# RWKV-7 chunk inverses on VectorE in a PSUM bank, merged in place by 32-row tiles, and token-shift mixes kept in DRAM

## The chip, the cores and the metric

The kernel runs on one core of a Trainium2 chip. The metric is the device time of one execution in microseconds. PE is TensorE, DVE is VectorE, ACT is ScalarE, POOL is GpSimd, and SP is the engine whose queue issues the transfers. Each engine works through its own instructions in order; a wait holds all that stand behind it on that engine.

## The reference

Two layers over 512 tokens of width 1024, in float32. Layer 0 is RWKV-7 time mixing with 16 heads of 64, layer 1 differential attention; both end with a gated per-layer embedding. The change lies in layer 0:

```python
xmix = xn[None] + (x_prev - xn)[None] * mu[:, None, None, :]
rkvg = jnp.einsum('cbsd,cde->cbse', xmix[:4], w_in)
r, k, v, g = rkvg[0], rkvg[1], rkvg[2], rkvg[3]
...
def step(state, inp):
    r_t, w_t, k_t, v_t, kk_t, a_t = inp
    s_kk = jnp.einsum('bhij,bhj->bhi', state, kk_t)
    state = (state * w_t[:, :, None, :]
             - s_kk[..., None] * (kk_t * a_t)[:, :, None, :]
             + v_t[..., None] * k_t[:, :, None, :])
    return state, jnp.einsum('bhij,bhj->bhi', state, r_t)
```

## The kernel before

**Dense work.** A float32 product is made of three fast matmuls (`mm3`, L277 to L279) of values split into a high and a low part. The four projections r, k, v, g of layer 0 have two halves of 512 output columns each; `ORDER` lists the eight. Each half takes eight steps over the input width, one step four groups of three 128x512 matmuls. A step needs a split weight tile (`w_split`: a copy on ACT or DVE by L262, then the low part by L310 on POOL or DVE) and a mix. `mix` forms x + (x_prev - x) mu for 128 channels: ACT scales into a PSUM bank (L472), DVE adds the shifted term there (L474), ACT copies the high part (L478), DVE forms the low part (L480). Both halves of a projection form the same mix anew, 64 in all; two buffers for even and two for odd steps hold them.

**Chunks.** The recurrence goes in chunks of 64 tokens, eight of them, for two groups of eight heads. `gram` forms for two chunks at once the masked products of keys and queries, in G. Each chunk and head then needs the inverse of a 64x64 unit triangular matrix. `inverse` makes 32 of them at once (four chunks of one group), so there are four calls, here numbers 0 and 1 (group 0), 2 and 3 (group 1). Each 64x64 matrix has two 32x32 diagonal blocks and one below. The diagonal blocks are inverted by substitution, 31 steps of one multiplication (L903) and one addition (L906), all blocks side by side; `SUBST` gives the engine: POOL for 0, 1 and 2, DVE for 3. DVE brings blocks into and out of that layout by 32x32 transposes (L895, L912, L929). Then the block below is made by two products ("merge", L947 and L960), with operands set into zeroed 64-wide tiles (memsets L934 to L937 on POOL, copies on ACT), and the result is put together in a tile X.

**Recurrence.** For each chunk PE runs L1033 (state), L1043 (G), L1059 (the inverse X), L1072 (state update) and L1078 (output), with copies on ACT between (L1056, L1064, L1098) and the state's update on DVE (L1092, L1095). `finish` normalises and gates a block of 128 tokens and head group (L1118 to L1168, DVE and POOL).

**Order.** All work is written as generators. `Streams` runs a plan while the program is built: each step yields an engine and a cost, the earliest start goes next, and the order in which steps are taken is the order of the instructions on each engine. Where a step may go to either of two engines, `PREF` is an allowance for the first one. After the projections come, on one stream, the embedding's product, the output projection and layer 1.

Of the kernel before, what the change touches and what calls it, by code (L numbers as in the profile page):

```python
# [198 lines left out]
def yoco_kernel(ctx: ExitStack, tc: tile.TileContext, I, out):  # L199
    nc = tc.nc  # L200
    k = Core(tc, ctx)
    cp = k.const
# [56 lines left out]
    ENG = {"ACT": nc.scalar, "DVE": nc.vector, "Pool": nc.gpsimd}  # L259

    def copy(dst, src):
        (nc.scalar.copy if sc.eng == "ACT" else ENG[sc.eng].tensor_copy)(dst, src)  # L262
# [197 lines left out]
    def mix(key, hf, par):  # L460

        c = MIX[key]
        for d in range(par, NT, 2):
# [8 lines left out]
            nc.scalar.activation(m, x_at(d), AF.Copy, scale=omm[:, c, d : d + 1])  # L472
# [1 line left out]
            nc.vector.scalar_tensor_tensor(  # L474
                m[:, 1:], x_at(d)[:, 0 : S - 1], vcol(V_MU + c, d), m[:, 1:], ALU.mult, ALU.add
            )
# [1 line left out]
            nc.scalar.copy(h, m)  # L478
# [1 line left out]
            nc.vector.tensor_sub(l, m, h.bitcast(F32))  # L480
# [389 lines left out]
    def inverse(n):  # L870

        g, cp = batches[n]
        for u in range(2):
# [13 lines left out]
        for q, r in enumerate(quads):  # L887
            for hd, src in lower(q, 32 * (q % 2)):
                yield "ACT/DVE+", (0.24, 0.2)
                copy(na[r, hd], src)  # L890
# [6 lines left out]
        eng = SUBST[g][cp]  # L897
        ve = ENG[eng]
        base, rate = {"DVE": (0.19, 0.00105), "Pool": (0.21, 0.0024)}[eng]
        for s_ in range(31):  # L900
# [2 lines left out]
            ve.tensor_mul(  # L903
                tmp[:, 0:m, 0:w], bc(xs[:, s_ : s_ + 1, 0:w], [P, m, w]), bc(nb[:, s_ + 1 : 32, s_ : s_ + 1], [P, m, w])
            )
            ve.tensor_add(xs[:, s_ + 1 : 32, 0:w], xs[:, s_ + 1 : 32, 0:w], tmp[:, 0:m, 0:w])  # L906
# [5 lines left out]
        nc.vector.transpose(xr, bc(xs.unsqueeze(3), [P, 32, 16, 2]))  # L912
# [17 lines left out]
        yield "take", "R", 3  # L930
        bdc, bdw = R([P, 16, HN]), R([P, 16, HN])
        Xc = X[g, cp] = R([P, 16, HN])
        yield "Pool", 0.89
# [4 lines left out]
        for par in range(2):
            q, c0 = 2 - 2 * par, 32 * (1 - par)
            for hd, src in lower(q, 32):  # L940
                yield "ACT/DVE+!", (0.24, 0.2)
                copy(bdc[quads[q], hd, c0 : c0 + 32], src)
        yield "take", "pw", 1
        ps = bank("pw")
        yield "PE", 1.67, 0.5
        for hd in range(16):
            nc.tensor.matmul(ps[0:64, 32 * hd : 32 * hd + 32], bdc[:, hd, :], xT[:, hd, :], start=True, stop=True)  # L947
        yield "ACT", 1.18
        for j in range(2):
            nc.scalar.copy(bdw[quads[2 * j + 1], :, quads[j]], pv_(ps, 32)[quads[j]])  # L950
        yield "free", "pw", 1
        yield "free", "R", 2
        yield "ACT!", 2.5
        for j, q in enumerate(quads):
            nc.scalar.copy(Xc[q, :, 32 * (j % 2) : 32 * (j % 2) + 32], x32[q])
        yield "take", "pw", 1
        ps = bank("pw")
        yield "PE", 1.67, 0.5
        for hd in range(16):
            nc.tensor.matmul(ps[0:64, 32 * hd : 32 * hd + 32], bdw[:, hd, :], x32[:, hd, :], start=True, stop=True)  # L960
        yield "ACT", 1.18
        for j in range(2):
            nc.scalar.copy(Xc[quads[2 * j], :, 32:64], pv_(ps, 32)[quads[j]])
        yield "free", "pw", 1
        yield "free", "H", 2
# [828 lines left out]
```

## Time and profile before

| | us |
|---|---|
| median of 3 runs (lowest, highest) | 887.76 (884.79, 887.78) |
| profiled execution | 888.55 |
| its span | 886.8 |

The span runs from the first to the last instruction; 1.75 us of the profiled time lie around it. In the views, each engine's busy time does not count waits; a wait is put down to what ended it, so "PE p L279 <- POOL R L310" is time in which PE stood at line 279 until POOL's instruction of line 310 was done. "PEclk" is the granted TensorE clock as a share of full speed. Tiles H and R are buffers in SBUF, p is a PSUM bank, RAW an unsplit weight.

### The profile page before, as it was taken

What the parts mean: (1) busy time and instruction counts of PE and PEld (TensorE: products, weight loads), DVE (VectorE), ACT (ScalarE), POOL (GpSimd) and SP (SyncE); (2) the same over time, 40 slices, a digit from 0 to 9 for tenths busy, and PEclk for the clock granted to TensorE, in tenths of its full rate; (3) what the DMA queues carried; (4) which work ended last, traced back from release to release, by engine and by line L of the source; (5) the groups of instructions that cost most, each with busy time, mean ns of one, the idle gap of its engine ahead of it and who ended that gap; (6) DMA issues with size and microseconds to landing.
All of it is one profiled execution on the core that took longest, in us unless ns stands there. A gap on an engine that the chain in (4) does not pass through costs nothing.

```text
span 886.8 us, 13629 instructions
## 1 busy us (share of the span) xinstructions
PE 809.3 (91%) x4968; PEld 666.3 (75%) x4968; DVE 614.0 (69%) x1243; ACT 515.0 (58%) x1135; POOL 304.3 (34%) x419
## 2 busy tenths in 40 slices
PE   6989999079999997679999999999999999999996
PEld 3767776057888886567878888888888888888885
DVE  3999987177665889895636668548886268863744
ACT  3888569158654775345634456449775378753531
POOL 3545418994251788674520001002100012210100
PEclk9998999579999997799999999999999999999998
DMA  7331220031121144025514444332022321324402
GB/s 284 106 96 60 74 95 0 0 127 42 61 72 49 60 159 138 1 72 193 163 56 147 141 127 158 95 95 67 30 95 72 96 71 50 101 90 157 140 14 95
DMA packets 31203, 83.12 MB, mean 94 GB/s; under 512 B 4128, under 2 KB 8608, under 8 KB 31136
## 3 DMA queue, kind: packets, MB, share of 16 engines
q1 hardware_dynamic: 31136, 82.25, 28.3%
q8 instruction: 39, 0.64, 0.3%
q14 instruction: 28, 0.23, 0.1%
HBM read 73.85 MB, written 8.39 MB: 93 GB/s over the span
## 4 chain that ended last, share of the span: by engine, by line
PE 68%; DVE 14%; POOL 7%; ACT 6%; issue 3%; DMA 2%; DVEq 0%; SPq 0%; POOLq 0%
PE p L277 16%; PE p L279 16%; PE p L278 16%; POOL H L906 2%; POOL H L903 2%; PE p L1600 2%; PE p L848 2%; PE p L1043 1%; PE p L1033 1%; PE p L1267 1%; ACT R L262 1%; PE p L1565 1%; PE p L1059 1%; PE p L1564 1%; DVE p L474 1%
## 5 line engine op out<-in xcount | busy, mean ns | idle before, releaser
L279 PE MATMUL p<-R,R 128*128 128x512 f32 x800 | 316.4, 396 | 25.5 <-POOL R L310 25.3
L277 PE MATMUL p<-R,R 128*128 128x512 f32 x800 | 328.7, 411 | 4.3 <-ACT R L478 2.0
L278 PE MATMUL p<-R,R 128*128 128x512 f32 x800 | 315.2, 394 | 3.7 <-DVE R L480 3.6
L279 PEld LDWEIGHTS p<-R,R 128*128 128x128 f32 x800 | 151.8, 190 | 60.1 <-POOL R L310 26.2
L277 PEld LDWEIGHTS p<-R,R 128*128 128x128 f32 x800 | 152.2, 190 | 36.7 <-ACT R L478 3.6
L278 PEld LDWEIGHTS p<-R,R 128*128 128x128 f32 x800 | 152.3, 190 | 31.7 <-DVE R L480 5.2
L310 POOL TENSOR_TENSOR R<-RAW,R 128x512 fp32r<-128x512 f32 x46 | 63.5, 1386 | 112.5 <-ACT R L262 61.3
L310 DVE TENSOR_TENSOR R<-RAW,R 128x512 fp32r<-128x512 f32 x94 | 67.4, 728 | 27.3 <-ACT R L262 25.2
L316 DVE SCALAR_TENSOR_TENSOR R<-RAW,vec,R 128x512 fp32r<-128x512 f32 x64 | 46.5, 747 | 32.0 <-ACT R L314 31.7
L262 ACT CAST R<-RAW 128x512 fp32r<-128x512 f32 x102 | 61.5, 619 | 5.4 <-DMA RAW<-in_w_v 2.2
L1254 POOL TENSOR_TENSOR hr<-hm,half 128x1 f32<-128x1 f32 x16 | 11.1, 693 | 147.8 <-DVE hm L1252 147.8
L474 DVE SCALAR_TENSOR_TENSOR p<-R,vec,p 128x511 f32<-128x511 f32 x64 | 48.1, 756 | 12.2 <-ACT p L472 11.9
L478 ACT CAST R<-p 128x512 fp32r<-128x512 f32 x64 | 37.7, 589 | 31.4 <-DVE p L474 30.8
L480 DVE TENSOR_TENSOR R<-p,R 128x512 fp32r<-128x512 f32 x64 | 43.4, 682 | 7.7 <-ACT R L478 7.5
L903 POOL TENSOR_TENSOR H<-H,R 128x126 f32<-128x126 f32 (+22 forms) x93 | 40.0, 430 | 24.4 <-PE p L664 20.7
L472 ACT ACTIVATE p<-R,omm 128x512 f32<-128x512 f32 x64 | 44.4, 693 | 3.4 <-DVE R L452 2.3
L314 ACT ACTIVATE R<-RAW,vec 128x512 fp32r<-128x512 f32 x64 | 44.6, 723 | 2.6 <-DMA RAW<-in_b_w_in 2.1
L906 POOL TENSOR_TENSOR H<-H,H 128x126 f32<-128x126 f32 (+22 forms) x93 | 39.2, 422 | 7.3
L1576 ACT ACTIVATE H<-p,mx 128x128 f32<-128x128 f32 (+3 forms) x64 | 33.4, 527 | 8.0 <-DVE mx L1573 6.4
L1569 DVE CUSTOM_DVE_ANT_0 p<-p,cmask 128x128 f32<-128x128 f32 (+3 forms) x64 | 30.5, 506 | 6.9 <-PE p L1565 6.7
L262 ACT CAST R<-R 64x512 fp32r<-64x512 f32 (+1 forms) x37 | 22.9, 618 | 20.9 <-DVE R L1160 16.4
L996 ACT COPY R<-p 128x128 f32<-128x128 f32 x64 | 12.3, 278 | 35.3 <-PE p L993 35.2
(225 smaller groups left out, 1453.9 us busy)
## 6 DMA issues: line engine op xcount, KB each, us to landing
RAW<-in_ple_gate SPq DMA_DIRECT2D x16, 512.0 KB, 3.5
RAW<-in_kv_w SPq DMA_DIRECT2D x16, 512.0 KB, 3.4
RAW<-in_b_w_in SPq DMA_DIRECT2D x16, 512.0 KB, 3.5
R<-in_x SPq DMA_DIRECT2D x8, 512.0 KB, 5.9
RAW<-in_w_r SPq DMA_DIRECT2D x8, 512.0 KB, 3.4
RAW<-in_w_k SPq DMA_DIRECT2D x8, 512.0 KB, 3.4
RAW<-in_w_v SPq DMA_DIRECT2D x8, 512.0 KB, 3.4
RAW<-in_w_g SPq DMA_DIRECT2D x8, 512.0 KB, 3.4
```

What stands on the lines that cost most here:

```text
L262: (nc.scalar.copy if sc.eng == "ACT" else ENG[sc.eng].tensor_copy)(dst, src)
L277: nc.tensor.matmul(ps, ah, bh, start=first, stop=False)
L278: nc.tensor.matmul(ps, ah, bl, start=False, stop=False)
L279: nc.tensor.matmul(ps, al, bh, start=False, stop=last)
L310: ENG[sc.eng].tensor_sub(lo, f, hi.bitcast(F32))
L314: nc.scalar.activation(hi, f, AF.Copy, scale=g)
L316: nc.vector.scalar_tensor_tensor(lo, f, g, hi.bitcast(F32), ALU.mult, ALU.subtract)
L472: nc.scalar.activation(m, x_at(d), AF.Copy, scale=omm[:, c, d : d + 1])
L474: nc.vector.scalar_tensor_tensor(m[:, 1:], x_at(d)[:, 0 : S - 1], vcol(V_MU + c, d), m[:, 1:], ALU.mult, ALU.add)
L480: nc.vector.tensor_sub(l, m, h.bitcast(F32))
L903: ve.tensor_mul(tmp[:, 0:m, 0:w], bc(xs[:, s_ : s_ + 1, 0:w], [P, m, w]), bc(nb[:, s_ + 1 : 32, s_ : s_ + 1], [P, m, w]))
L906: ve.tensor_add(xs[:, s_ + 1 : 32, 0:w], xs[:, s_ + 1 : 32, 0:w], tmp[:, 0:m, 0:w])
```

## The change

Three parts, and two settings of the plan.

- **Substitution.** Numbers 0, 2 and 3 run on DVE, number 1 on POOL. On DVE the unknowns `xs` lie in a PSUM bank (ACT copies the identity there), so that each of the 62 instructions has one input in the bank and one in SBUF, and the additions write to the bank.
- **Merge.** The zeroed tiles, the memsets and X are gone. Each merge is 32 products of 32x32 blocks (two for each matrix pair, in different rows and columns of the array) where it was 16 of 128x64 by 32, taken from G and from the substitution's result as they lie. The inverse is written back into G, by 16 copies of 32x128 on ACT or DVE and 8 on ACT, and the recurrence reads it there (L1059 becomes L1081).
- **Mixes.** The first half of each projection forms its mixes and stores each to DRAM (`mD`, 512 KB each, 32 stores); the second half loads them (32 loads).
- **Plan.** v's first half now comes before r's second; `PREF` is 0; POOL's cost in the substitution is raised.

```diff
-ORDER = [("r", 0), ("k", 0), ("r", 1), ("v", 0), ("k", 1), ("v", 1), ("g", 0), ("g", 1)]
+ORDER = [("r", 0), ("k", 0), ("v", 0), ("r", 1), ("k", 1), ("v", 1), ("g", 0), ("g", 1)]
+FIRST = [(k, h) for n, (k, h) in enumerate(ORDER) if k not in [x for x, _ in ORDER[:n]]]
-PREF = 0.4
+PREF = 0.0
-SUBST = (("Pool", "Pool"), ("Pool", "DVE"))
+SUBST = (("DVE", "Pool"), ("DVE", "DVE"))
...
+            if (key, hf) not in FIRST:
+                yield "wait", ("kept", key, d)
+                yield "DMA", 1.7
+                nc.sync.dma_start(t.bitcast(F32), mD[c, d])
+                yield "set", ("mix", key, hf, d)
+                continue
...
             yield "set", ("mix", key, hf, d)
+            yield "DMA!", 1.7
+            nc.sync.dma_start(mD[c, d], t.bitcast(F32))
+            yield "set", ("kept", key, d)
...
+        if eng == "DVE":
+            yield "take", "pw", 1
+            eye, xs = xs, bank("pw").rearrange("p (s c) -> p s c", c=16)
+            yield "ACT!", 0.52
+            nc.scalar.copy(xs, eye)
...
-        nc.gpsimd.memset(bdc, 0.0)
-        nc.gpsimd.memset(bdw, 0.0)
-        nc.gpsimd.memset(Xc, 0.0)
...
-            nc.tensor.matmul(ps[0:64, 32 * hd : 32 * hd + 32], bdc[:, hd, :], xT[:, hd, :], start=True, stop=True)
+            for j in range(2):
+                block = lower(2 * j, hd // 8, hd // 4 % 2)[:, hd % 4, 32:64]
+                nc.tensor.matmul(
+                    ps[j][quads[2 * j + 1], 32 * hd : 32 * hd + 32], block, xT[quads[2 * j], hd, :], start=True, stop=True
+                )
...
+        for u in range(2):
+            for hh in range(2):
+                sl = slice(8 * u + 4 * hh, 8 * u + 4 * hh + 4)
+                for q in range(4):
+                    yield "ACT/DVE+!", (0.2, 0.2)
+                    copy(lower(q, u, hh)[:, :, 32 * (q % 2) : 32 * (q % 2) + 32], x32[quads[q], sl])
```

The plan comes out in another order. On DVE, where substitution 0 ends, before (L474 and L480 are mixes, L586 to L590 centre v; H_1073 holds the unknowns that POOL works on):

```order
L480 TENSOR_TENSOR R_1422<-p_1423,R_1422 128x512 [waits PE_49,Activation_49]
L474 SCALAR_TENSOR_TENSOR p_1452<-R_113,vec_83,p_1452 128x511 [waits Activation_49]
L480 TENSOR_TENSOR R_1451<-p_1452,R_1451 128x512 [waits PE_49,Activation_49]
L912 STREAM_TRANSPOSE R_1523<-H_1073 128x1024 [waits DMAHW5_49,Pool_49]
L586 TENSOR_REDUCE vmean_88<-H_1524 128x8 [waits Activation_49]
L586 TENSOR_REDUCE vmean_88<-H_1528 128x8 [waits Activation_49]
L588 TENSOR_SCALAR vmean_88<-vmean_88 128x8
L590 TENSOR_TENSOR H_1432<-H_1432,vmean_88 128x512 [waits DVE_49]
```

and in the changed kernel (p_1011 is the bank, L923 and L926 are the substitution, L313 a weight split, L932 to L943 bring the result back):

```order
L923 TENSOR_TENSOR H_1001<-p_1011,R_1102 128x3x15 [waits DVE_49]
L926 TENSOR_TENSOR p_1011<-p_1011,H_1001 128x3x15 [waits DVE_49]
L923 TENSOR_TENSOR H_1001<-p_1011,R_1102 128x2x15 [waits DVE_49]
L926 TENSOR_TENSOR p_1011<-p_1011,H_1001 128x2x15 [waits DVE_49]
L313 TENSOR_TENSOR R_1445<-RAW_1303,R_1445 128x512 [waits Activation_49]
L923 TENSOR_TENSOR H_1001<-p_1011,R_1102 128x16 [waits DVE_49]
L926 TENSOR_TENSOR p_1011<-p_1011,H_1001 128x16 [waits DVE_49]
L932 STREAM_TRANSPOSE R_1476<-p_1011 128x1024 [waits DMAHW1_49,DMAHW7_49,DVE_49,PE_49]
L941 TENSOR_SCALAR H_1489<-R_1476,rowm_100 128x32x16 [waits DVE_49]
```

The transpose of the result waited for POOL with v's and the next mixes behind it; now it follows the substitution on DVE itself, with weight splits between the last steps, and no mixes stand there.

On SP, before, while v's first half is loaded (L293 loads a weight, L561 one of the decay's):

```order
L293 DMA RAW_899<-in_w_v 128x1024 [waits DMAHW3_49,DVE_49,Pool_49]
L293 DMA RAW_928<-in_w_v 128x1024 [waits DMAHW4_49,DVE_49,Pool_49]
L293 DMA RAW_975<-in_w_v 128x1024 [waits DMAHW6_49,DVE_49,Pool_49]
L293 DMA RAW_1000<-in_w_v 128x1024 [waits DMAHW7_49,Pool_49]
L293 DMA RAW_1052<-in_w_k 128x1024 [waits DMAHW0_49,DVE_49,Activation_49]
L561 DMA H_1120<-in_w2a 128x512
```

and in the changed kernel while r's second half is loaded (L296 loads a weight, L493 stores a mix, L475 loads one):

```order
L493 DMA mD<-R_959 128x1024 [waits DMAHW7_49,DVE_49]
L296 DMA RAW_1042<-in_w_r 128x1024 [waits DMAHW4_49,Activation_49,Pool_49]
L475 DMA R_1051<-mD 128x1024 [waits DMAHW1_49,PE_49]
L493 DMA mD<-R_1007 128x1024 [waits DVE_49]
L475 DMA R_1088<-mD 128x1024 [waits DMAHW3_49,PE_49]
L296 DMA RAW_1111<-in_w_k 128x1024 [waits DMAHW6_49,DVE_49,Pool_49]
```

Between two weight loads now stand stores that wait for DVE and loads of mixes that wait for PE to free their buffer.

On PE, in one step of group 1's recurrence, before, between the product with G (L1043) and the product with the inverse (L1059); L993 and L1154 are transposes for other chunks:

```order
L1043 MATMUL p_3509<-R_3414,R_2550 64x64
L993 MATMUL p_3519<-ident_85,R_1190 128x128
L993 MATMUL p_3519<-ident_85,R_1195 128x128
L993 MATMUL p_3519<-ident_85,R_1374 128x128
L993 MATMUL p_3519<-ident_85,R_1709 128x128
L1154 MATMUL p_3533<-ident_85,R_2194 128x128 x4
L1059 MATMUL p_3509<-H_3529,R_3249 64x64 x8
```

and in the changed kernel, between the same two (L1065 and L1081), during g's first half (L280 to L282 are the dense matmuls):

```order
L1065 MATMUL p_3164<-R_2511,R_2390 64x64
L280 MATMUL p_2863<-R_2980,R_2787 128x512
L281 MATMUL p_2863<-R_2980,R_2787 128x512
L282 MATMUL p_2863<-R_2980,R_2787 128x512
L280 MATMUL p_2841<-R_2994,R_2837 128x512
L281 MATMUL p_2841<-R_2994,R_2837 128x512
L282 MATMUL p_2841<-R_2994,R_2837 128x512
L1081 MATMUL p_3164<-H_3181,R_2389 64x64
```

Group 1's recurrence stands beside g's two halves now, where before most of it stood after them; so dense matmuls of g lie between its products.

More of the change, by code (lines that the diff above doesn't have):

```diff
@@ L49 @@
 INVP = (0.5, 0.5, 0.5, 0.5)
-SUBST = (("Pool", "Pool"), ("Pool", "DVE"))
+SUBST = (("DVE", "Pool"), ("DVE", "DVE"))
+RUN = ((1, 1), (1, 1))
 QP, UEP, L1P, PLEP = 4, 5, 7, 8
@@ L212, in yoco_kernel @@
     hD = dram.tile([NB, P, D], F32, name="hD")
+    mD = dram.tile([4, NT, P, 2, S], F32, name="mD")
     ring = ctx.enter_context(pool("ring"))
@@ L818, in yoco_kernel @@
     AOFF, ROFF = (64, 0), (0, 64)
-    G, X, UV, YT = {}, {}, {}, {}
+    G, UV, YT = {}, {}, {}
     heads = [(ii, hh) for ii in range(4) for hh in range(2)]
@@ L872, in inverse, with lower @@
         g, cp = batches[n]
-        for u in range(2):
-            yield "wait", ("gram", 2 * cp + u, g)
-        def lower(q, c):
+        def lower(q, u, hh):
             par = 1 - q // 2
-            off = AOFF[par] + c
-            for n, (u, hh) in enumerate(((0, 0), (0, 1), (1, 0), (1, 1))):
-                yield slice(4 * n, 4 * n + 4), G[2 * cp + u, hh, g][quads[q], :, par, off : off + 32]
+            return G[2 * cp + u, hh, g][quads[q], :, par, AOFF[par] : AOFF[par] + HN]
+        yield "wait", ("gram", 2 * cp, g)
+        eng = SUBST[g][cp]
+        ve = ENG[eng]
         yield "take", "H", 3
@@ L886, in inverse @@
         nc.sync.dma_start(xs, I["eye32"])
[L887 to L890, printed above, removed]
+        if eng == "DVE":
+            yield "take", "pw", 1
+            eye, xs = xs, bank("pw").rearrange("p (s c) -> p s c", c=16)
+            yield "ACT!", 0.52
+            nc.scalar.copy(xs, eye)
+            yield "free", "H", 1
+        for u in range(2):
+            yield "wait", ("gram", 2 * cp + u, g)
+            for hh in range(2):
+                for q, r in enumerate(quads):
+                    yield "ACT/DVE+!", (0.2, 0.2)
+                    copy(na[r, 8 * u + 4 * hh : 8 * u + 4 * hh + 4], lower(q, u, hh)[:, :, 32 * (q % 2) : 32 * (q % 2) + 32])
         yield "take", "R", 1
@@ L896, in inverse @@
         yield "free", "H", 1
-        eng = SUBST[g][cp]
-        ve = ENG[eng]
-        base, rate = {"DVE": (0.19, 0.00105), "Pool": (0.21, 0.0024)}[eng]
+        base, rate = {"DVE": (0.19, 0.00105), "Pool": (0.24, 0.0024)}[eng]
+        late = 0.09 if eng == "DVE" else 0.08
+        cost = [2 * base + 2 * rate * (31 - s_) * (s_ // 2 + 1) for s_ in range(31)]
         for s_ in range(31):
             m, w = 31 - s_, s_ // 2 + 1
-            yield eng + "+", 2 * base + 2 * rate * m * w - base / 2
+            if s_ % RUN[g][cp] == 0:
+                yield "DVE" if eng == "DVE" else "Pool+", sum(cost[s_ : s_ + RUN[g][cp]]) - late
             ve.tensor_mul(
@@ L912, in inverse @@
         nc.vector.transpose(xr, bc(xs.unsqueeze(3), [P, 32, 16, 2]))
-        yield "free", "H", 1
-        yield "take", "H", 2
-        x32, xT = HT([P, 16, 32]), HT([P, 16, 32])
+        yield ("free", "pw", 1) if eng == "DVE" else ("free", "H", 1)
+        yield "take", "H", 3
+        x32, xT, w32 = (HT([P, 16, 32]) for _ in range(3))
         xv = x32.rearrange("p h t -> p t h")
@@ L925, in inverse @@
         fl = lambda t: t.rearrange("p a j -> p (a j)")
-        pv_ = lambda ps, j: ps.rearrange("p (a j) -> p a j", j=j)
         yield "DVE", 0.6
         nc.vector.transpose(fl(xT), fl(x32))
[L930 to L933, printed above, removed]
-        nc.gpsimd.memset(bdc, 0.0)
-        yield "Pool!", 1.78
-        nc.gpsimd.memset(bdw, 0.0)
-        nc.gpsimd.memset(Xc, 0.0)
[L938 to L942, printed above, removed]
@@ L943, in inverse @@
-        yield "take", "pw", 1
-        ps = bank("pw")
+        yield "take", "pw", 2
+        ps = [bank("pw") for _ in range(2)]
         yield "PE", 1.67, 0.5
         for hd in range(16):
-            nc.tensor.matmul(ps[0:64, 32 * hd : 32 * hd + 32], bdc[:, hd, :], xT[:, hd, :], start=True, stop=True)
+            for j in range(2):
[3 more added lines that the diff above has]
+                )
@@ L948, in inverse @@
         yield "ACT", 1.18
         for j in range(2):
[L950 to L957, printed above, removed]
+            r = quads[2 * j + 1]
+            nc.scalar.copy(w32[r], ps[j][r].rearrange("p (a j) -> p a j", j=32))
@@ L958, in inverse @@
+        yield "free", "pw", 2
+        yield "take", "pw", 2
+        ps = [bank("pw") for _ in range(2)]
         yield "PE", 1.67, 0.5
         for hd in range(16):
[L960 to L965, printed above, removed]
+            for j in range(2):
+                r = quads[2 * j + 1]
+                nc.tensor.matmul(
+                    ps[j][quads[2 * j], 32 * hd : 32 * hd + 32], w32[r, hd, :], x32[r, hd, :], start=True, stop=True
+                )
@@ new lines, in inverse @@
+        for u in range(2):
+            for hh in range(2):
+                sl = slice(8 * u + 4 * hh, 8 * u + 4 * hh + 4)
+                for q in range(4):
+                    yield "ACT/DVE+!", (0.2, 0.2)
+                    copy(lower(q, u, hh)[:, :, 32 * (q % 2) : 32 * (q % 2) + 32], x32[quads[q], sl])
+        for u in range(2):
+            for hh in range(2):
+                sl = slice(8 * u + 4 * hh, 8 * u + 4 * hh + 4)
+                for j in range(2):
+                    yield "ACT!", 0.2
+                    nc.scalar.copy(
+                        lower(2 * j, u, hh)[:, :, 32:64], ps[j][quads[2 * j]].rearrange("p (a j) -> p a j", j=32)[:, sl]
+                    )
@@ L966, in inverse @@
+        yield "free", "pw", 2
+        yield "free", "H", 3
         yield "set", ("prep", g, cp)
@@ L1059, in recur @@
                 nc.tensor.matmul(
-                    pA[U, cols(ii, hh)], X[g, cq // 2][:, 8 * (cq % 2) + 4 * hh + ii, :], gt[:, cols(ii, hh)],
+                    pA[U, cols(ii, hh)], G[cq, hh, g][:, ii, par, AOFF[par] : AOFF[par] + HN], gt[:, cols(ii, hh)],
                     start=True, stop=True, skip_group_check=True,
```

3 lines of the change are left out of this document (removed).

## The prediction

> **What bounds the kernel now.** I read the busy shares and slices of the page first, then busy time by stage, then who made PE wait in the two stages that stand out.
>
> ```profile
> PE 809.3 (91%) x4968; PEld 666.3 (75%) x4968; DVE 614.0 (69%) x1243; ACT 515.0 (58%) x1135; POOL 304.3 (34%) x419
> PE   6989999079999997679999999999999999999996
> ```
> PE is the bound over the whole, with two holes: slices 7 and 8 (155 to 200 us) and 15 to 17 (333 to 399). By stage (columns: length, busy us of PE, PEld, DVE, ACT, POOL with instruction counts, then the granted clock, DMA share and GB/s):
>
> ```profile
> 20.00:100.00 80.00, 72.54 (x328) 56.81 (x327) 78.64 (x112) 62.10 (x112) 39.59 (x32) 0.96 0.23 73
> 140.00:160.00 20.00, 14.59 (x59) 10.16 (x57) 12.50 (x18) 16.50 (x34) 17.69 (x40) 0.96 0.00 0
> 160.00:180.00 20.00, 2.26 (x5) 1.83 (x6) 4.35 (x8) 0.00 (x0) 18.20 (x47) 0.50 0.06 18
> 180.00:200.00 20.00, 13.96 (x77) 10.74 (x75) 13.83 (x22) 11.86 (x31) 18.61 (x31) 0.77 0.36 127
> 200.00:320.00 120.00, 117.85 (x1110) 100.37 (x1109) 86.69 (x148) 77.60 (x178) 56.60 (x90) 1.00 0.21 64
> 340.00:360.00 20.00, 11.68 (x119) 10.83 (x120) 19.45 (x39) 9.45 (x22) 15.86 (x15) 0.57 0.12 41
> 360.00:380.00 20.00, 14.30 (x145) 12.66 (x144) 15.57 (x37) 7.22 (x19) 9.44 (x11) 0.84 0.00 1
> 380.00:400.00 20.00, 15.40 (x164) 12.70 (x163) 19.47 (x36) 9.25 (x25) 16.86 (x15) 0.93 0.26 81
> 100.00:409.00 309.00, 257.33 (x2083) 213.31 (x2083) 229.03 (x388) 181.16 (x405) 185.25 (x295) 0.91 0.23 73
> 440.00:880.00 440.00, 437.19 (x2262) 366.31 (x2261) 279.10 (x684) 245.03 (x568) 52.48 (x61) 1.00 0.30 96
> ```
> Hole A (140 to 200): 5.4+17.7+6.0 = 29.2 us idle, and the busy part at clocks 0.96, 0.50 and 0.77 loses 0.6+1.1+3.2 = 4.9 more: 34. Hole B (340 to 400): 18.6 idle and 5.0+2.3+1.1 = 8.4 by the clock: 27. With dense work beside a recurrence (200 to 320) only 2.2 of 120 is idle, and nothing is to be had after 440.
>
> Two marks in time, group 0's first recurrence matmul and the first dense one after the gates:
>
> ```profile
> 205.83 1.15 PE L1043 MATMUL p<-R,R 128*64 128x64 f32 x16
> 409.30 0.40 PE L277 MATMUL p<-R,R 128*128 128x512 f32 x1
> ```
> Hole A, PE's and DVE's longest waits (total, times, longest) and POOL's rows around them:
>
> ```profile
> PE p L279 <- POOL R L310: 25.3, 2, 20.5
> DVE R L912 <- POOL H L906: 20.6, 2, 19.5
> 130.30 0.29 POOL L903 TENSOR_TENSOR H<-H,R 128x31 f32<-128x31 f32 x1 [20.66 <-PE p L664]
> 175.33 0.22 POOL L906 TENSOR_TENSOR H<-H,H 128x16 f32<-128x16 f32 x1
> 176.42 1.27 POOL L310 TENSOR_TENSOR R<-RAW,R 128x512 fp32r<-128x512 f32 x1
> ```
> Substitution 0 runs on POOL from 130.30 to 175.55, interleaved with number 1. A weight split (L310) stands behind it, and PE waits for that split; DVE stands at the transpose L912, with the mixes queued behind. Hole B:
>
> ```profile
> PE p L1072 <- ACT R L1064: 5.0, 3, 3.7
> PE p L1033 <- DVE R L1095: 4.7, 4, 1.5
> PE p L947 <- ACT R L262: 3.1, 1, 3.1
> ```
> These are links of group 1's recurrence. Each step of it is a chain of small products, copies and state updates, PE has too little dense work to put between them, and its clock falls as well (0.57 from 340 to 360), which makes the small products slower still.
>
> **The change, part by part.** *Substitution 0 to DVE.* In DVE's order, shown with the change, the transpose L912 waited for POOL; as L932 it follows DVE's own last addition, and weight splits stand inside the substitution. Hole A goes whole: -34. DVE's price comes from these rows (timeline: start, length; then groups: busy, mean ns; then min/median/max ns):
>
> ```profile
> 362.25 0.28 DVE L903 TENSOR_TENSOR H<-H,R 128x120 f32<-128x120 f32 x1
> 362.57 0.28 DVE L906 TENSOR_TENSOR H<-H,H 128x120 f32<-128x120 f32 x1
> 387.48 0.17 DVE L903 TENSOR_TENSOR H<-H,R 128x16 f32<-128x16 f32 x1
> 387.69 0.17 DVE L906 TENSOR_TENSOR H<-H,H 128x16 f32<-128x16 f32 x1
> L906 DVE TENSOR_TENSOR H<-H,H 128x126 f32<-128x126 f32 (+22 forms) x31 | 18.4, 595 | 1.1
> L903 DVE TENSOR_TENSOR H<-H,R 128x126 f32<-128x126 f32 (+22 forms) x31 | 13.8, 444 | 0.4
> L310 DVE TENSOR_TENSOR R<-RAW,R x94: 641/691/1540, 40.9 to 855.3; 128x512 fp32r<-128x512 f32 x94
> L480 DVE TENSOR_TENSOR R<-p,R x64: 637/684/694, 25.2 to 345.2; 128x512 fp32r<-128x512 f32 x64
> L474 DVE SCALAR_TENSOR_TENSOR p<-R,vec,p x64: 710/746/1373, 22.8 to 342.9; 128x511 f32<-128x511 f32 x64
> L704 DVE SCALAR_TENSOR_TENSOR R<-H,H x8: 661/683/1719, 55.3 to 208.7; 128x512 f32<-128x512 f32 x8
> ```
> Undisturbed, one starts 0.32 us after the last at 120 elements and 0.21 at 16: 0.193 + 0.00105 per element. With 62 instructions and 5,712 elements that is 18.0 us. The one substitution that DVE ran took 18.4+13.8 = 32.2, since POOL was working beside it. With one input in a bank L480 never passed 0.694, where L310, both inputs in SBUF, reached 1.540; so I expect the undisturbed price, plus 0.063 for each of the 31 additions written back to the bank (L474's 746 against L704's 683): 20 us. Bounds 18 and 32; I take the value near the lower end because the row nearest in kind, L480, is the one that POOL doesn't stretch.
>
> [...]
>
> *Mixes from DRAM.* Of 64 mixes 32 go:
>
> ```profile
> L474 DVE SCALAR_TENSOR_TENSOR p<-R,vec,p 128x511 f32<-128x511 f32 x64 | 48.1, 756 | 12.2 <-ACT p L472 11.9
> L480 DVE TENSOR_TENSOR R<-p,R 128x512 fp32r<-128x512 f32 x64 | 43.4, 682 | 7.7 <-ACT R L478 7.5
> hD<-R SPq DMA_DIRECT2D x4, 512.0 KB, 2.6
> R<-hD SPq DMA_DIRECT2D x4, 512.0 KB, 5.5
> ```
> DVE loses 32 x 1.438 = 46 us, gains 3x20-32 = 28 for the substitutions, and some 22 operations of 0.69 that POOL did (15): -3, so about 226 us of work in a stage 36 shorter than 309, 83% full. That is hidden behind PE, not a gain of its own. Before 100 us nothing changes: the first 24 mixes are still formed, and DVE is full (78.64 of 80). The 64 added transfers of 512 KB go through SP's queue (its order is shown with the change). Weights and fetches now stand behind stores that wait for DVE. A fetch lands in some 5.5 us, and PE has three steps of twelve 0.23 us matmuls (8.2 us) before it needs it, so it costs nothing unless SP is held over 2.7 us; I take 0 to 10, inside the new waits below.
>
> *Merges by 32-row tiles.* PE issues 64 instructions of 32x32 for 32 before, eight times:
>
> ```profile
> 195.03 2.02 PE p L947 x32
> 219.93 0.62 PE p L1072 x16
> ```
> L1072 alternates between halves of the array, 0.039 apiece in its run; L947, which doesn't, 0.063. So 64 cost 2.5 to 4.0 us, 0.5 to 2.0 more, in all +4 to +16, all on PE. I take +10, since successive tiles differ but change weights each time. POOL's twelve memsets and ACT's part of 32 mixes go too; neither engine is waited for there any more, so I cost that at nothing.
>
> *Recurrence earlier.* In PE's order before, small matmuls alone stand between L1043 and L1059 of a group 1 step; after it, six dense ones stand between L1065 and L1081. These (1.4 us) now cover the copy that L1059 waited for. So B behaves like 200 to 320: -27.
>
> *New waits.* PE stands at four merges, as it stood 3.1 us at L947. Copies into G now follow each second merge, 24 small ones before the recurrence starts. And substitution 1 stays on POOL, with its L932 on DVE ahead of key and split work:
>
> ```profile
> L903 POOL TENSOR_TENSOR H<-H,R 128x126 f32<-128x126 f32 (+22 forms) x93 | 40.0, 430 | 24.4 <-PE p L664 20.7
> L906 POOL TENSOR_TENSOR H<-H,H 128x126 f32<-128x126 f32 (+22 forms) x93 | 39.2, 422 | 7.3
> ```
> That is at least 31 x 0.852 = 26 us on POOL, and 45 if as stretched as number 0 was. I take +15 for all of it (four merges at about 2.5, and 5 for SP and L932); ends 4 and 30.
>
> Sum against the profiled execution, 888.55 (span 886.8 and 1.75 around it): 888.5-34-27+10+15 = 852.5. The median of the runs is 0.8 lower, so 852.
>
> **Rivals.** *DVE becomes the bound* (slower). If its substitutions cost 32 as the traced one did, DVE has 226+36 = 262 us; at 83% full the stage takes 316 instead of 309, and the time is 888+7 = 895. For it speaks DVE's 98% before 100 us, against it L480's steady 0.69. It decides from about 31 us each.
> *Hole B stays*: the recurrence is bound by its own links whatever stands between: 852+27 = 879. Against it speaks 200 to 320, where steps with dense work cost no idle time.
> *POOL's remaining substitution holds DVE*: hole A moves to L932 of number 1, at up to the 19.5 us seen: 872. The order puts two state updates ahead of it, which speaks against.
> *No new waits, and merges no dearer*: 888-61+4 = 831, down to 826 with nothing at all left over. [...]
>
> **How the numbers follow.** Likeliest (838 to 866, predicted 852): 0.50. No new waits (826 to 838): 0.18. Hole B stays or L932 holds (866 to 883): 0.20. Both, about as before: 0.05. DVE-bound: 0.07. The range 826 to 882 leaves about 0.15 out. A change of 0.5%, 4.4 us, is about what a measurement can tell from none: faster 0.88, same 0.05, slower 0.07.
>
> **What would show it.** Right: no PE wait for a POOL split near 160; L923+L926 on DVE at 0.27 to 0.35 us each and none over 0.7; the first recurrence matmul, at 205.8 before, near 165; the dense work after the gates, at 409.3 before, from about 373; merges of 64 in 2.5 to 4 us. Wrong: the substitutions near 0.5 us an instruction; DVE idle behind POOL at L932; PE waiting for DMA into a mix; or PE at clock 0.5 to 0.8 anywhere between 140 and 370.

## The result, and the profile after

The changed kernel takes 855.1 us (median of 4 runs, 852.11 to 855.45) beside 886.4 us for the kernel before on the same chip: a ratio of 0.964, 95% interval 0.961 to 0.967. The prediction was 852. The profiled execution took 855.45 us, span 853.7. PE's rows of the page:

```profile
PE 810.8 (95%) x5224; PEld 668.3 (78%) x5224; DVE 614.7 (72%) x1399; ACT 461.9 (54%) x1051; POOL 200.5 (23%) x250
PE   6897999999899699898999999999999999999996
```
The two holes have closed; what is left are single slices of 6 to 8 tenths, spread out. Busy time by stage (columns as in the prediction):

```profile
20.00:100.00 80.00, 69.24 (x262) 53.83 (x261) 71.48 (x102) 56.41 (x99) 28.17 (x25) 0.86 0.53 191
100.00:140.00 40.00, 40.00 (x250) 32.50 (x249) 35.01 (x76) 20.12 (x44) 9.94 (x9) 0.93 0.60 209
160.00:180.00 20.00, 20.00 (x216) 16.23 (x215) 14.80 (x22) 14.13 (x35) 18.07 (x34) 1.00 0.58 219
220.00:240.00 20.00, 18.05 (x177) 15.21 (x178) 13.64 (x29) 13.49 (x36) 3.50 (x4) 0.66 0.46 146
280.00:300.00 20.00, 13.36 (x67) 9.70 (x65) 18.61 (x48) 7.51 (x16) 6.36 (x7) 0.82 0.59 218
340.00:360.00 20.00, 17.20 (x245) 14.79 (x244) 11.37 (x16) 11.76 (x37) 14.58 (x15) 0.91 1.03 344
380.00:400.00 20.00, 17.22 (x143) 14.30 (x143) 16.13 (x28) 8.90 (x19) 9.23 (x10) 0.91 0.44 144
```
From 160 to 180, where PE had 2.26 us of work before, it has 20.00. But 20 to 100 is worse than before (69.24 at clock 0.86, where 72.54 at 0.96 stood), and there are new dents at 220 and 280. Adding idle time and what the clock takes from the busy time, as the prediction did for its two holes, over all windows (20 to 100, 100 to 140, then by 20 us) gives a loss for each stage, which serves for the experiments as well. The stages are fixed stretches of time, so work that moves earlier moves from one column to another. One of the ten executions of xs_in_sbuf (902.05 us) ran in a slower state of the chip and is left out of its median.

| lost us of PE in | 20-100 | 100-140 | 140-200 | 200-280 | 280-340 | 340-440 | sum | median us | ratio to before (95%) |
|---|---|---|---|---|---|---|---|---|---|
| before | 10.4 | 0.0 | 34.1 | 2.1 | 1.7 | 29.0 | 77.3 | 886.4 | |
| after | 20.5 | 2.8 | 0.0 | 8.4 | 11.9 | 9.7 | 53.4 | 855.1 | 0.964 (0.961-0.967) |
| null_plan | 20.4 | 0.8 | 0.0 | 13.0 | 19.0 | 8.6 | 61.8 | 866.6 | 0.975 (0.972-0.979) |
| two_fewer_r | 20.4 | 3.6 | 2.4 | 3.4 | 20.0 | 11.0 | 60.9 | 862.5 | 0.971 (0.967-0.975) |
| stores_later | 20.3 | 8.6 | 6.9 | 1.7 | 18.9 | 7.9 | 64.4 | 865.8 | 0.973 (0.968-0.979) |
| subst2_on_pool | 17.5 | 0.0 | 0.5 | 8.3 | 20.4 | 7.8 | 54.5 | 859.9 | 0.967 (0.959-0.974) |
| g0_before_v1 | 19.9 | 1.6 | 1.3 | 4.9 | 32.0 | 6.7 | 66.4 | 867.6 | 0.977 (0.973-0.980) |
| pref_as_before | 16.3 | 0.0 | 0.0 | 12.4 | 16.8 | 20.7 | 66.2 | 873.2 | 0.981 (0.975-0.988) |
| subst0_on_pool | 19.8 | 4.8 | 24.4 | 3.7 | 14.2 | 4.2 | 71.1 | 874.8 | 0.985 (0.980-0.989) |
| subst_as_before | 19.9 | 1.6 | 24.1 | 7.0 | 11.4 | 9.7 | 73.8 | 878.2 | 0.989 (0.985-0.993) |
| old_merges | 20.4 | 2.8 | 0.5 | 17.3 | 21.5 | 15.2 | 77.8 | 882.0 | 0.993 (0.990-0.996) |
| third_half_r1 | 16.4 | 5.5 | 30.8 | 5.8 | 11.9 | 9.7 | 80.0 | 882.5 | 0.995 (0.992-0.997) |
| all_mixes_formed | 18.6 | 8.4 | 13.2 | 18.0 | 13.0 | 13.3 | 84.5 | 886.9 | 0.999 (0.997-1.002) |
| xs_in_sbuf | 20.5 | 2.8 | 4.4 | 19.0 | 31.2 | 17.3 | 95.2 | 892.8 | 1.005 (1.001-1.008) |

The sum follows the time: 24 of the 33 us between the two profiled executions lie in it, some 7 more in shorter merges, which are no idle time (below), and 2 behind 440. Idle time and clock have different shares. From 20 to 100 the changed kernel has 10.8 us idle (7.5 before) and loses 9.7 by the clock (2.9 before); from 200 to 280 it has 2.3 us idle and loses 6.1 by the clock. Columns rest on one profiled execution each, and kernels that share all settings that bear on a stage still differ in it: by 3 us from 20 to 100 (17.5 to 20.5), by more elsewhere.

The parts that the prediction spoke of: substitutions on DVE (the two groups, then the busy time of L923 and of L926 in two of the three stretches in which DVE substituted), a merge and the instruction behind it, the first recurrence matmul, the first dense one after the gates, and the transfers:

```profile
L926 DVE TENSOR_TENSOR p<-p,H 128x126 f32<-128x126 f32 (+22 forms) x93 | 24.4, 263 | 3.2
L923 DVE TENSOR_TENSOR H<-p,R 128x126 f32<-128x126 f32 (+22 forms) x93 | 23.4, 252 | 1.2
130.00:162.00 32.00, 7.94 (x31) 1.00 0.74 256
...
306.00:336.00 30.00, 7.78 (x31) 1.00 0.52 176
...
130.00:162.00 32.00, 8.15 (x31) 1.00 0.74 256
...
306.00:336.00 30.00, 8.14 (x31) 1.00 0.52 176
```
```profile
167.81 1.20 PE L955 MATMUL p<-H,R 32*32 32x32 f32 x64
168.94 0.50 PE L280 MATMUL p<-R,R 128*128 128x512 f32 x1
...
178.45 0.74 PE L1065 MATMUL p<-R,R 128*64 128x64 f32 x9
...
397.11 0.80 PE L280 MATMUL p<-R,R 128*128 128x512 f32 x1
```
```profile
mD<-R SPq DMA_DIRECT2D x32, 512.0 KB, 3.6
R<-mD SPq DMA_DIRECT2D x32, 512.0 KB, 5.7
```
A substitution is 16 us of DVE (7.94 + 8.15 for the first one); its instructions take 0.257 us on average beside work of POOL (79 of them) and 0.258 apart from it (107). A merge is recorded as 64 instructions on PE, 32 before; it holds PE for 1.13 us, from 167.81 to the next start at 168.94.

### The profile page after: what moved, and what is told of

Read it like the earlier page. It is cut to its first block, busy times and chain, and to the rows that moved or that the text cites. A ratio compares the mean times of both kernels' runs of the same rounds, so it can differ in the third digit from the quotient of the medians.

```text
span 853.7 us, 14158 instructions
## 1 busy us (share of the span) xinstructions
PE 810.8 (95%) x5224; PEld 668.3 (78%) x5224; DVE 614.7 (72%) x1399; ACT 461.9 (54%) x1051; POOL 200.5 (23%) x250
## 4 chain that ended last, share of the span: by engine, by line
PE 83%; DVE 10%; ACT 3%; issue 2%; DMA 1%; POOL 1%; DVEq 0%; POOLq 0%; SPq 0%; ACTq 0%
PE p L280 20%; PE p L282 19%; PE p L281 19%; PE p L1620 2%; PE p L1081 2%; PE p L1065 2%; PE p L860 2%; PE p L1055 1%; PE p L1585 1%; PE p L1287 1%; PE p L754 1%; PE p L1584 1%; PE p L1100 1%; PE p L1611 1%; PE p L785 1%
## 5 line engine op out<-in xcount | busy, mean ns | idle before, releaser
L280 PE MATMUL p<-R,R 128*128 128x512 f32 x800 | 329.9, 412 | 5.3 <-ACT R L487 2.7
L282 PE MATMUL p<-R,R 128*128 128x512 f32 x800 | 317.5, 397 | 1.3 <-DVE R L313 1.3
L280 PEld LDWEIGHTS p<-R,R 128*128 128x128 f32 x800 | 153.2, 192 | 37.4 <-ACT R L487 4.1
L282 PEld LDWEIGHTS p<-R,R 128*128 128x128 f32 x800 | 153.1, 191 | 35.3 <-DVE R L313 1.7
L313 DVE TENSOR_TENSOR R<-RAW,R 128x512 fp32r<-128x512 f32 x105 | 71.4, 694 | 30.4 <-ACT R L265 29.3
L313 POOL TENSOR_TENSOR R<-RAW,R 128x512 fp32r<-128x512 f32 x35 | 46.9, 1346 | 146.0 <-ACT R L265 88.0
L265 ACT CAST R<-RAW 128x512 fp32r<-128x512 f32 x103 | 62.0, 619 | 10.2 <-issue 4.8
L276 POOL TENSOR_TENSOR orr<-orm,half 128x4 f32<-128x4 f32 x8 | 9.6, 1201 | 142.7 <-DVE orm L274 137.9
L1307 ACT COPY R<-p 128x512 f32<-128x512 f32 x16 | 9.4, 588 | 45.6 <-PE p L282 45.3
L1375 DVE SCALAR_TENSOR_TENSOR R<-H,R 128x512 f32<-128x512 f32 x16 | 11.1, 692 | 24.9 <-ACT H L1368 24.9
L869 DVE TENSOR_TENSOR R<-p,cmk 128x512 f32<-128x512 f32 x32 | 21.1, 682 | 9.9 <-PE p L860 9.9
L1368 ACT ACTIVATE H<-p 128x512 f32<-128x512 f32 x16 | 9.6, 597 | 34.0 <-PE p L282 34.0
L481 ACT ACTIVATE p<-R,omm 128x512 f32<-128x512 f32 x32 | 22.1, 694 | 10.7 <-DVE R L455 3.7
L487 ACT CAST R<-p 128x512 fp32r<-128x512 f32 x32 | 18.6, 587 | 16.3 <-DVE p L483 15.9
L926 DVE TENSOR_TENSOR p<-p,H 128x126 f32<-128x126 f32 (+22 forms) x93 | 24.4, 263 | 3.2
```

The costliest lines, as they stand in the source:

```text
L280: nc.tensor.matmul(ps, ah, bh, start=first, stop=False)
L282: nc.tensor.matmul(ps, al, bh, start=False, stop=last)
L313: ENG[sc.eng].tensor_sub(lo, f, hi.bitcast(F32))
L869: nc.vector.tensor_mul(G[cq, hh, g][:, 2 * p2 : 2 * p2 + 2].rearrange("p a b c -> p a (b c)"), pg[hh].rearrange("p (a b) -> p a b", b=2 * ...
```

## The experiments

Each edit makes the planner build a new order of everything behind it, so the first question is what a new order is worth by itself.

**null_plan.**

```diff
-    LATENCY = {..., "DVE": 0.13, ...}
+    LATENCY = {..., "DVE": 0.14, ...}
```


> The changed kernel with one number of the planner's table moved by a hair (DVE's latency 0.13 to 0.14): the same work on the same engines, but a newly made order. It measures what a new order alone is worth. Theory P (much of what the undone parts lost is a less lucky order, not the part itself): 865 to 885. Theory R (the losses are the parts' own resources): 850 to 862.

Measured: 866.6, 11.5 us slower than the changed kernel (10 by the ratios, since the kernel before was 1.6 us slower in that session too), with no part of the change touched. Theory P is right as far as this one new order goes: a difference under some 12 us from 855 proves nothing by its time alone. What is claimed below rests on a stage of the trace beside the time.

**two_fewer_r.**

```diff
-    N_R, N_H = 44 - N_RAW, 11
+    N_R, N_H = 42 - N_RAW, 11
```


> The changed kernel with 40 instead of 42 of the 4 KB tiles R, about what the inverses' own tiles X and the merges' two zeroed tiles held in the old merges. Theory R (the old merges lost 27 us because they held tiles that splits and mixes wait for): 870 to 885, with the idle places near 220 to 240 and 280 to 320 again. Rival (the old merges lose by their PE, POOL and ACT work): 855 to 860.

Measured: 862.5, inside what null_plan moved. Two tiles fewer don't make the loss of the old merges (below); theory R falls.

**subst0_on_pool** and **subst_as_before.** The two kernels differ in one line:

```diff
-SUBST = (("DVE", "Pool"), ("DVE", "DVE"))
+SUBST = (("Pool", "Pool"), ("DVE", "DVE"))   # subst0_on_pool
+SUBST = (("Pool", "Pool"), ("Pool", "DVE"))  # subst_as_before
```


> The changed kernel with substitution 0 alone back on POOL (numbers 2 and 3 stay on DVE). Theory 1 (substitution 0 on POOL made the hole from 140 to 200): the hole comes back between 140 and 200, 20 to 34 us slower, 875 to 889, with PE waiting for a POOL split or DVE standing at the transpose L932 behind POOL. Rival (room on DVE made the gain, whatever engine substitutes): DVE has 18 us less to do, 850 to 860.

> The changed kernel with substitutions 0, 1 and 2 on POOL and only number 3 on DVE, as before; mixes in DRAM, order of halves and merges as changed. Theory 1 (POOL's substitutions made both holes): 885 to 895, both holes back. Rival (the saved mix work and the tiles set free are a gain of their own): DVE has 36 us less to do, 860 to 875.

With number 0 on POOL the stage and DVE's longest wait read:

```profile
160.00:180.00 20.00, 1.86 (x64) 1.81 (x64) 6.57 (x11) 0.45 (x3) 18.10 (x43) 0.61 0.06 23
...
DVE R L932 <- POOL H L926: 28.4, 2, 27.4
PE p L955 <- DVE H L947: 18.7, 1, 18.7
```
(The last line is PE's longest wait.) Hole A is back at its place (1.86 us busy; 24.4 of the 34.1 us lost from 140 to 200) with the wait that the prediction named: the transpose at DVE's head, behind POOL's last addition. That is shown by the trace; the times, 874.8 and 878.2, agree. PE, though, doesn't stand at a weight split of POOL's, as it did before for 20.5 us, but at its merge (L955), whose operand DVE makes behind that transpose (L947); the other half of the prediction's account, the split, is not tested by itself. Hole B didn't come back with substitution 2 on POOL as well (9.7 lost from 340 to 440, as in the changed kernel), so theory 1 is right for A and wrong for B. And mixes, merges and order without substitutions 0 and 2 on DVE still leave a gain of 1% (0.985 to 0.993).

**third_half_r1** and **pref_as_before.** These undo the plan's two settings, each alone:

```diff
-ORDER = [("r", 0), ("k", 0), ("v", 0), ("r", 1), ...]
+ORDER = [("r", 0), ("k", 0), ("r", 1), ("v", 0), ...]   # third_half_r1
-PREF = 0.0
+PREF = 0.4                                              # pref_as_before
```


> The changed kernel with the old order of the halves (r0, k0, r1, v0, ...), so that r's kept mixes are read back at once. Theory D (the new order slows the first stage): third half from 80 us instead of 97.7, busy PE from 20 to 100 back to 72 and more, 845 to 860. Theory C (PREF does): the stage stays slow, third half after 90 us, 855 to 870.

> The changed kernel with PREF back at 0.4: of the engines that may do a copy or a split, the planner prefers the first named one unless the other ends 0.4 us sooner. The stage from 20 to 100 us lost its 3 us of busy PE, and clock, also in the kernel without stores, so it is not the stores. Theory C (PREF 0 is what slows the first stage): splits go back to POOL (15 in the stage, as before, where the changed kernel has 11), busy PE from 20 to 100 back to 72, third half from 80 to 85, and 845 to 856 in all. Rival D (the order of the halves is): the stage stays at 69 and under, 855 to 870.

The stage from 20 to 100 of the one and of the other, then the old order's from 140 to 200, and two waits of PE (total of the run, times, longest) whose longest lies in it:

```profile
20.00:100.00 80.00, 71.47 (x301) 57.11 (x299) 74.30 (x108) 54.12 (x97) 28.11 (x25) 0.89 0.55 200
```
```profile
20.00:100.00 80.00, 70.02 (x295) 53.70 (x293) 74.51 (x104) 58.55 (x103) 39.20 (x34) 0.91 0.56 204
```
```profile
140.00:160.00 20.00, 12.10 (x98) 9.39 (x98) 18.47 (x43) 11.65 (x22) 10.06 (x22) 0.76 0.36 133
160.00:180.00 20.00, 18.16 (x128) 14.05 (x127) 12.26 (x18) 16.48 (x39) 17.95 (x33) 0.89 0.14 53
180.00:200.00 20.00, 5.51 (x47) 4.72 (x47) 12.86 (x26) 2.10 (x10) 11.20 (x21) 0.70 0.64 212
...
PE p L1065 <- DMA R<-vcD: 14.5, 1, 14.5
PE p L955 <- DVE H L947: 8.1, 2, 7.6
```
Each kernel lost 4 us less in the first stage, of the 10 that it lost more than before, and the third half started at 83.6 and 84.0 us, not 97.7. That shows neither theory: stores_later and all_mixes_formed, below, start it at 83.0 and 80.1 with both settings as changed, and subst2_on_pool, with both as changed too, lost 3 us less. What slows the first stage stays open, and both theories were wrong on the time. The old order loses 30.8 us from 140 to 200 although DVE substitutes. With v fourth its mixes are formed in the same stretch as the substitution, PE stands 7.6 us at the merge behind it, and the recurrence then waits 14.5 us for v's own values (vcD). With v third, a half with fetched mixes stands there and v is long done. So, in these kernels, hole A closed only by the substitution and the new order together.

**stores_later.** The store goes from `mix` to the dense step that takes the mix:

```diff
             m = mixes[key, hf, d]
+            if (key, hf) in FIRST:
+                yield "DMA!", 1.7
+                nc.sync.dma_start(mD[MIX[key], d], m.bitcast(F32))
+                yield "set", ("kept", key, d)
```


> The changed kernel with each mix's store issued from SP when the dense step takes the mix, not when the mix is made. Theory A (from 20 to 140 us weight loads stand on SP behind stores that wait for DVE): SP's waits at the store fall under 10 us, busy PE from 20 to 100 rises from 69 toward 72.5, the third half starts some 5 to 10 us sooner, the time is 843 to 850. Rival B (it is the halves' new order, or the DMA traffic itself, that starves PE there): same, 853 to 858, with the stage as slow as before.

SP's longest wait from 20 to 140 (total, times, longest), and the stage:

```profile
SPq L363 <- DVE R L493: 51.5, 21, 6.7
...
20.00:100.00 80.00, 66.31 (x270) 52.13 (x268) 75.80 (x107) 54.63 (x97) 29.44 (x26) 0.90 0.57 204
```
The edit failed in its aim: SP still waits for DVE at the store, 51.5 us where it was 35.5, probably because PE's step is planned ahead of the time at which DVE delivers. It tells nothing against theory A. The next kernel does.

**all_mixes_formed.**

```diff
-FIRST = [(k, h) for n, (k, h) in enumerate(ORDER) if k not in [x for x, _ in ORDER[:n]]]
+FIRST = list(ORDER)
...
-            yield "DMA!", 1.7
-            nc.sync.dma_start(mD[c, d], t.bitcast(F32))
-            yield "set", ("kept", key, d)
```


> The changed kernel, but all 64 mixes are formed by ACT and DVE and none is stored or loaded; order of the halves, substitutions and merges as changed. Theory 1 (the gain is that POOL's substitutions no longer hold DVE and the splits; the mixes in DRAM only make room on DVE): DVE has 32 x 1.44 = 46 us more to do in a stage that it fills to some 83%, SP loses its 64 transfers, so part of the gain goes, some 5 to 20 us: 860 to 875. Rival (the gain is the mix work saved): 32 us or more go, 885 or above. If SP's queue costs more than the mixes save: below 855.

Its first stage, the stage of DVE's first substitution, and PE's longest wait:

```profile
20.00:100.00 80.00, 67.50 (x283) 52.15 (x281) 75.76 (x108) 56.04 (x99) 31.37 (x26) 0.91 0.20 66
...
140.00:160.00 20.00, 11.34 (x65) 8.28 (x64) 18.47 (x55) 8.06 (x23) 7.91 (x8) 0.74 0.41 132
...
PE p L281 <- DVE R L489: 15.1, 6, 8.7
```
Without a single store the first stage is still slow (18.6 lost), so the stores don't make it. The whole gain of the change is gone (0.997 to 1.002), the rival's number, not theory 1's. Of the 31 us that the table counts more than for the changed kernel, 13 lie from 140 to 200, where DVE substitutes and forms mixes together (18.47 of 20 us busy, PE waiting 8.7 us for a mix's low part), and 10 from 200 to 280; a new order by itself can move some 12. So room on DVE is no by-product here: in this kernel nothing of the gain is left without it.

**xs_in_sbuf.**

```diff
-        if eng == "DVE":
-            yield "take", "pw", 1
-            eye, xs = xs, bank("pw").rearrange("p (s c) -> p s c", c=16)
-            yield "ACT!", 0.52
-            nc.scalar.copy(xs, eye)
-            yield "free", "H", 1
...
-        yield ("free", "pw", 1) if eng == "DVE" else ("free", "H", 1)
+        yield "free", "H", 1
```


> The changed kernel with DVE's three substitutions in SBUF instead of a PSUM bank; ACT's copy of the unit blocks goes and a bank is free. Theory S (both inputs in SBUF are stretched while POOL works): the two lines on DVE go from 0.26 to 0.4 us and more on average while POOL's substitution runs, each substitution from 17 to 20-30 us, the time 860 to 880. Rival (the bank is the scarcer thing: mixes, grams and operands wait for one): durations within 10%, the time 845 to 855.

The two groups; the stage that lost most, and PE's longest wait, which ended after it; then two rows of DVE and two of POOL, from shortly before it:

```profile
L920 DVE TENSOR_TENSOR H<-H,H 128x126 f32<-128x126 f32 (+22 forms) x93 | 30.3, 326 | 3.2
L917 DVE TENSOR_TENSOR H<-H,R 128x126 f32<-128x126 f32 (+22 forms) x93 | 27.9, 300 | 0.7
...
300.00:320.00 20.00, 2.27 (x9) 1.43 (x8) 19.07 (x64) 3.97 (x16) 4.13 (x5) 0.58 0.27 92
...
PE p L949 <- DVE H L941: 16.4, 2, 14.4
```
```profile
290.44 1.22 DVE L920 TENSOR_TENSOR H<-H,H 128x96 f32<-128x96 f32 x1
294.44 1.14 DVE L917 TENSOR_TENSOR H<-H,R 128x126 f32<-128x126 f32 x1
...
290.27 1.28 POOL L313 TENSOR_TENSOR R<-RAW,R 128x512 fp32r<-128x512 f32 x1 [7.70 <-ACT R L265]
294.16 1.27 POOL L313 TENSOR_TENSOR R<-RAW,R 128x512 fp32r<-128x512 f32 x1 [2.61 <-ACT R L265]
```
An instruction of 0.26 us that meets one of POOL's on the way can end just after it (290.44 + 1.22, POOL 290.27 + 1.28). Of the 186, 35 overlap work of POOL and take 0.56 us on average, the other 151 take 0.26; 19 of the 35 are stretched, and each of these ends within 0.2 us after POOL's. In the bank 79 overlap and 107 don't, and both take 0.26. So theory S is right in kind: 58.2 us of DVE in all for 47.8. Its means stay below the 0.4 it gave, since POOL is seldom at work there, and the time is above its range. But those 10 us more on DVE are not most of the 38. From 300 to 320 substitutions 2 and 3 take 14.5 of DVE's 19.07 us, partly in turns, and PE, with 2.27 us of work, waits 7.7 us for a mask (L869) and 14.4 at its merge (L949), for an operand that DVE makes after the substitution. What part of that is the stretching and what the new order, no run separates.

**old_merges.** The changed kernel's merges replaced by the code of before (diff above, read backwards).

> The changed kernel with the merges of before: 32 matmuls 64 wide with zeroed blocks from POOL's memsets, and the inverse in a tile of its own. [...] Rival (copies back into G and four banks make the merges a cost): faster, 845 to 852.

PE's waits at the first product of its merges:

```profile
PE p L972 <- DVE R L265: 7.9, 3, 5.3
PE p L972 <- POOL H L769: 1.7, 1, 1.7
```
Measured: 882.0, 27 us above the changed kernel, so the rival falls. Shorter merges are worth 8 x 0.8 us (1.13 for 1.95). And PE waits 9.6 us at the merges, most of it for the copies into the zeroed tiles, which stand last before the merge on DVE (L265), where the changed kernel's merges wait 1.7 us in all. What is left, some 12 us, is what a new order can move; how much of the waiting the copies themselves make is not separated. From 200 to 440 PE also waits for a mix (L489, 7.7 us) and a weight split on DVE (L313, 4.2); R tiles are not it (two_fewer_r).

**subst2_on_pool** and **g0_before_v1** went for the dent from 280 to 340, which is new in the changed kernel and deeper in most of the others (11 to 32 us lost, 1.7 before).

```diff
-SUBST = (("DVE", "Pool"), ("DVE", "DVE"))
+SUBST = (("DVE", "Pool"), ("Pool", "DVE"))   # subst2_on_pool
-..., ("k", 1), ("v", 1), ("g", 0), ("g", 1)]
+..., ("k", 1), ("g", 0), ("v", 1), ("g", 1)] # g0_before_v1
```


> The changed kernel with substitution 2 on POOL and 0 and 3 on DVE. Every kernel with group 1's substitutions on DVE has a hole of 5 to 10 us between 280 and 340, with DVE 95% busy and POOL 25%. Theory E (DVE is the bound there, since the mixes of g's first half, group 1's masks and the substitutions meet on it): the hole shrinks to under 3 us, 845 to 856. Rival (DVE then stands at the transpose L932 behind POOL, as for substitution 0): a wait of DVE for POOL of 10 us and more, 865 to 880.

> The changed kernel with one swap in the order of the halves: g's first half, whose mixes DVE forms, before v's second, whose mixes are fetched (r0, k0, v0, r1, k1, g0, v1, g1). Theory F (a half whose mixes are formed must not run where DVE substitutes; the changed kernel lost 6.6 us of busy PE and some clock from 280 to 300 to just that, while DVE had 6 to 10 us of 20 free from 220 to 260): the hole from 280 to 340 closes to under 3 us, nothing as deep opens from 210 to 280, 842 to 852. Rival G (v's second half is needed for group 1's recurrence, which then starts late): small matmuls with idle PE from 380 on, 860 to 880. A newly made order alone, with nothing to it, has cost 7 to 11 us.

PE's rows of g0_before_v1 around the hole, and DVE's rows shortly before its end:

```profile
281.84 0.40 PE L282 MATMUL p<-R,R 128*128 128x512 f32 x1
300.79 1.43 PE L955 MATMUL p<-H,R 32*32 32x32 f32 x46 [18.55 <-DVE H L947]
```
```profile
294.77 0.28 DVE L926 TENSOR_TENSOR p<-p,H 128x115 f32<-128x115 f32 x1
294.97 0.16 DVE L923 TENSOR_TENSOR H<-p,R 128x16 f32<-128x16 f32 x1
295.17 0.18 DVE L926 TENSOR_TENSOR p<-p,H 128x16 f32<-128x16 f32 x1
295.26 0.26 DVE L923 TENSOR_TENSOR H<-p,R 128x110 f32<-128x110 f32 x1
```
The elements (115, 16, 110) tell it: substitutions 2 and 3 alternate on DVE, instruction by instruction, so the earlier one ends late, and PE stands 18.55 us at its first merge with dense work queued behind. Moving g's formed half away did not close the dent (32.0 lost), so theory F falls, and no small matmuls with idle PE appear from 380, so G does too. In subst2_on_pool the dent is deeper as well (20.4), so theory E falls; DVE never waits at L932 for POOL, so its rival falls too; PE stood 9.1 us at its merge, and 859.9 (0.959 to 0.974) can't be told from the changed kernel. The same wait at a merge, ahead of dense work in PE's queue, is in four more kernels: 18.7 and 18.9 us in subst0_on_pool and subst_as_before, 14.4 in xs_in_sbuf, 7.6 in third_half_r1. No run puts the merge behind that dense work, so what it would save is not shown. In the changed kernel itself there is no such wait: PE's waits from 280 to 300 are for mixes (L489, 3.4 us in two, and ACT's L487, 1.8) and a mask (L869, 1.5).

No kernel beat the changed one.

## Why the prediction was right, and where it was wrong

Its time held, 852 for 855, but three terms were off, by 17, 14 and 8 us, and all but cancelled. So the closeness of the number is luck; the main cause, hole A, is not.

- **Hole A, -34.** Measured 34.1 to 0.0. The cause named (POOL's substitution 0 ahead of DVE's transpose) is shown by subst0_on_pool, though PE then stands at its merge and not at a weight split. What the prediction lacked is that the new order of the halves was as necessary (third_half_r1, 30.8 lost), and that without the mixes 13.2 us of the hole are there again.
- **DVE's price, 20 us a substitution.** Measured 16.1 busy. The 20, with bounds of 18 and 32, counted from one start to the next, which adds some 0.03 us to each instruction, so the measured price is at the lower end. None took over 0.55 us: right to go by L480, too cautious with its 0.063 for writing to the bank. Undisturbed, the additions took 0.260 us in SBUF (76 of them in xs_in_sbuf) and 0.263 in the bank (53), the same instructions in both.
- **Mixes.** Right that PE never waited for a fetched mix (none for mD among its waits); a fetch landed in 5.7 us, 5.5 was expected. "Before 100 us nothing changes" was wrong by 10 us, 3 of idle time and 7 by the clock. The reason suspected, SP's queue behind the stores, isn't the cause (18.6 lost without a store); the cause stays open.
- **Merges, +10.** Wrong in sign: at full clock 1.13 us for 64 where 32 took 1.95 (from 195.03 to the next start, 196.98, in the kernel before), eight times: -7, outside the +4 to +16 given. The step that failed is the price per instruction, 0.039 to 0.063 from rows of wider tiles; 18 ns was measured. The waits for memsets and operand copies, which it put at nothing, count too: 9.6 us in old_merges, 1.7 here.
- **Hole B, -27.** 29.0 to 9.7 over 340 to 440: about -19. The recurrence's links that it named (L1072 and L1033, 9.7 us of PE's waits from 340 to 440) are down to 3.1 (L1055, as L1033 is now), which fits the account, but no run takes the dense work away from between them, so the cause stays unshown. Substitutions on POOL don't bring the hole back. PREF 0.4 loses 20.7 there, but half of it is another wait, 10.6 us for POOL's L1163.
- **New waits, +15.** They came to +29 by the table (20 to 140: +13, 200 to 280: +6, 280 to 340: +10), the upper end given. But only some 10 of it are idle time, near the 15 forecast; 20 are taken by the clock (0.86 from 20 to 100, 0.66 from 220 to 240, 0.82 from 280 to 300), which the sum counted in its two holes alone. So one of its own signs of being wrong, PE at a clock of 0.5 to 0.8 between 140 and 370, came true. And the waits were not at the sites named: no DVE wait at L932 for substitution 1, and PE's waits at merges are 1.7 us in all.

So -34, -19, -7 and +29 make -31, of 33 measured. The recurrence started at 178.4, not near 165, and the dense work after the gates at 397.1, not 373: recurrence work moved ahead of that mark (33 of its matmuls stand behind it, 248 before), and the waits and the clock took the rest. The rival DVE-bound, at 895, is near what xs_in_sbuf measured (892.8) with substitutions that POOL does stretch; but it stretches them by 3.5 us each, not by the 12 that the rival charged (32 for 20), so the number agrees and the mechanism isn't shown.

## What to carry to other kernels

When an order is planned, run one change that does nothing: here it moved the time by 10 to 11.5 us, about a third of the whole gain, and most single undoings must be read against it. Parts of such a change don't add: without the substitution, the fetched mixes or the halves' order, 20 to 32 us of a gain of 31 were lost each time, more than a new order moved. Read a loss by its two parts as well: where idle time falls the clock can still take some back, as it did here (20 us outside the old holes). And ask of each queue what stands at its head: in six of the kernels PE stood 7.6 to 18.9 us at a merge that waited for DVE, with dense work queued behind it.

## What the runs showed of the hardware that was not expected

- The merge's 32 products of 32x32, in two tiles with different rows and columns, recorded as 64 instructions, start in 1.13 us at full clock (167.81 to 168.94 in the changed kernel), 18 ns apiece. The 32 instructions of the wider tiles took 1.95 (195.03 to 196.98 in the kernel before), 61 apiece, and the prediction reckoned with 39 to 63.
- With one input in a bank the substitution's tensor-tensor operations on DVE took 0.26 us on average in the changed kernel whether POOL was at work beside them (79) or not (107). With both in SBUF, in xs_in_sbuf, they took 0.26 alone (151) and 0.56 on average beside POOL (35), and where they were stretched (19 of the 35) they ended up to 0.2 us after POOL's.
